# The section around the first five loads, synchronised by GpSimd in place of SyncE

## Chip, cores and metric

One core of a Trainium2 chip (trn2). The metric is device time in microseconds (us) of one execution; 298.03 us before, the median of three runs.

Engines are named as in the profile: PE is TensorE's matmul and PEld its weight load, DVE is VectorE, ACT ScalarE, POOL GpSimd, SP SyncE. A q behind a name (SPq, POOLq) stands for instructions that the engine's sequencer handles by itself: waits, no-ops, drains, branches and the issuing of transfers.

## What is computed

For every one of 8 batches and 12 heads, all dot products between 512 rows of x and 512 rows of y, each of 64 channels:

```python
def setup_inputs():
    batch, n_heads, seq_t, seq_s, channels = 8, 12, 512, 512, 64
    return {
        "x": np.random.randn(batch, n_heads, seq_t, channels).astype(np.float32),
        "y": np.random.randn(batch, n_heads, seq_s, channels).astype(np.float32),
    }

def reference(x: np.ndarray, y: np.ndarray) -> np.ndarray:
    return np.einsum('bhtc,bhsc->bhts', x, y).astype(np.float32)
```

Two inputs of 12.6 MB each are read and an output of 100.7 MB is written.

## The kernel before

**Tiling.** The 96 heads are taken in six groups of 16 (`NG` = 6). A group's x and y are each one load of 128 partitions by 4096 values (2 MB, `N` = 4096), so there are twelve loads: number 2g is x of group g, 2g + 1 is y of it. A head's 512 x 512 products make one result of 128 by 4096 floats (2 MB), in two halves of 2048, each from one of the two PSUM tiles `pm0` and `pm1`.

**Buffers.** Three buffers, `pair0` to `pair2`, hold two slots each. Five of the six slots (`SLOTS` = 5) take loads first and results later; the sixth holds group 1's inputs in bf16 at first. From the ninth result on, two results go out in one store of 4 MB from a pair.

**Stages of a group.** `compress` turns a landed load into bf16 (x by ACT into `xk`; y in four parts by DVE, POOL and ACT into `yb`), `mix` spreads x into `xb`, `transposes` on DVE makes `xT` and `yT`, PE makes the products in one loop (`all_products`), ACT copies them out of PSUM into slots (`copy`, line 140; the last result by DVE, line 142), and SP stores them (`transfer`, line 161).

**Who orders what.** Nearly all is ordered by hand: `emit` works out what an instruction has to wait for, puts the waits on its engine, and lets the instruction raise its engine's semaphore, or, for a transfer, the semaphore of its slot (`dma0` to `dma4`). All loads and nearly all stores are issued by SP on one DMA queue, in order; six pieces of one late store go by POOL's queue (`shares`).

**The beginning.** The framework opens the program with a barrier of all engines, in which POOL gathers the others' arrivals and then hands out the release (the trace puts it under line 430). Then comes the section that the change touches: `tc.tile_critical()`, line 367, in which five loads are issued (`load`, the issue itself is line 177). The section is a region that the framework's scheduler leaves alone; only the engines that have instructions in it, here SP, run into it. Around it the framework puts its own instructions, which the trace shows under lines 367 and 371: a no-op ahead of the section, which raises a semaphore; a branch into it that waits for this semaphore; behind the loads, on SP, a semaphore that SP raises, a drain that waits for that one and raises the first again, and a no-op that waits for the drain. The two no-ops stand in the queue of the section's synchronising engine, the argument `sync_engine`; where none is given, as here, they stand on SP. `tc.close()` ends the framework's part with a drain of all engines and two barriers (line 371), gathered by POOL again. All that follows is the hand-ordered part: the memsets of `xb` (line 378) and ACT's table load come first, then the first `compress`.

Of the kernel before, what the change touches and what calls it, by code (L numbers as in the profile page):

```python
# [9 lines left out]
def kernel(  # L10
# [13 lines left out]
    nc = tc.nc  # L24
# [148 lines left out]
    def load(n):  # L173
        i = loaded[n] = places[n]
        emit(
            "sp",
            lambda: nc.sync.dma_start(slots[i], (yv if n % 2 else xv)[n // 2]),  # L177
            writes=both(i),
            dma=i,
        )  # L180
# [183 lines left out]
            for part in range(4):  # L364
                mix(i + 1, "dve", part)

    with tc.tile_critical():  # L367
        for n in range(SLOTS):
            load(n)
    tc.close()  # L370
# [75 lines left out]
```

## Time and profile before

| what | value |
|---|---|
| median of three runs | 298.03 us (297.98 to 298.11) |
| the profiled execution's own time | 297.92 us |
| its span, first to last instruction | 296.1 us |
| granted TensorE clock, mean | 0.787 |
| busy: ACT, DVE, PE, POOL | 208.2, 158.0, 139.9, 59.5 us |
| bytes moved | 125.85 MB, 425 GB/s over the span |
| packets on SP's DMA queue, on POOL's | 5888, 288 |
| first load issued, first packet starts | 0.96 us, 1.99 us |
| first load landed (its semaphore complete) | 8.74 us |
| five loads' issue, each | 0.39 to 0.55 us |
| the closing barriers' last release | 4.30 us |

The span is measured from the first instruction to the last on the core; the execution's own time has some 1.8 us more around it. Starts are given from the span's beginning. The short instructions of the queues (no-ops, drains, waits) are read from the trace's instruction records, which have nanoseconds. A semaphore's update has a time of its own in the trace, apart from the instruction that makes it.

### The profile page before, as it was taken

What the parts mean: (1) busy time and instruction counts of PE and PEld (TensorE: products, weight loads), DVE (VectorE), ACT (ScalarE), POOL (GpSimd) and SP (SyncE); (2) the same over time, 40 slices, a digit from 0 to 9 for tenths busy, and PEclk for the clock granted to TensorE, in tenths of its full rate; (3) what the DMA queues carried; (4) which work ended last, traced back from release to release, by engine and by line L of the source; (5) the groups of instructions that cost most, each with busy time, mean ns of one, the idle gap of its engine ahead of it and who ended that gap; (6) DMA issues with size and microseconds to landing.
All of it is one profiled execution on the core that took longest, in us unless ns stands there. A gap on an engine that the chain in (4) does not pass through costs nothing.

```text
span 296.1 us, 1231 instructions
## 1 busy us (share of the span) xinstructions
PE 139.9 (47%) x404; PEld 37.9 (13%) x404; DVE 158.0 (53%) x76; ACT 208.2 (70%) x107; POOL 59.5 (20%) x29
## 2 busy tenths in 40 slices
PE   0000040437576557556654655577546646575400
PEld 0000010112111111111111111111111111121200
DVE  2167798899929594925808529258095240002600
ACT  1664666999999999666966696669666976684000
POOL 2399999992000000000000000000000000040000
PEclk9999995657779997778789776765798787756855
DMA  7999999999999999999999999999999999999998
GB/s 272 427 429 427 432 429 427 432 425 425 427 438 427 460 425 426 425 429 447 429 456 426 425 429 425 425 438 434 434 456 425 425 429 429 425 438 422 415 436 348
DMA packets 6178, 125.85 MB, mean 425 GB/s; under 512 B 896, under 2 KB 896, under 8 KB 932
## 3 DMA queue, kind: packets, MB, share of 16 engines
q1 hardware_dynamic: 5888, 125.03, 98.7%
q0 software_dynamic: 288, 0.80, 0.7%
q14 instruction: 2, 0.02, 0.0%
HBM read 25.17 MB, written 100.66 MB: 425 GB/s over the span
## 4 chain that ended last, share of the span: by engine, by line
DMA 56%; ACT 23%; PE 7%; issue 4%; DVE 3%; SPq 0%; ACTq 0%
DMA out_dram<-pair 43%; ACT pair L140 21%; DMA pair<-in_y_dram 7%; DMA pair<-in_x_dram 6%; PE pm L248 6%; DVE pair L142 3%; ACT xk L140 1%; PE pm L298 1%; ACT yb L140 1%; DVE xk L142 1%; SPq L177 0%; ACTq L92 0%; SPq L371 0%; SPq L367 0%
## 5 line engine op out<-in xcount | busy, mean ns | idle before, releaser
L248 PE MATMUL pm<-yT,xT 128*128 128x512 bf16 x384 | 136.6, 501 | 137.3 <-ACT pair L140 100.0
L140 ACT ACTIVATE pair<-pm 128x2048 f32<-128x2048 f32 x94 | 170.6, 1883 | 41.3 <-DMA out_dram<-pair 37.5
L225 DVE STREAM_TRANSPOSE xT<-xb 128x2048 uint32<-128x2048 uint32 x12 | 46.7, 3893 | 69.1 <-PE pm L248 66.7
L248 PEld LDWEIGHTS pm<-yT,xT 128*128 128x128 bf16 x384 | 36.0, 115 | 237.0 <-ACT pair L140 156.0
L161 POOL DMA_DIRECT2D out_dram<-pair x6 | 3.5, 583 | 193.7 <-ACT pair L140 193.7
L142 DVE COPY xb<-xk 32x2048 bf16<-32x2048 bf16 x32 | 41.7, 1304 | 0.9
L142 DVE CAST yb<-pair 64x2048 bf16<-64x2048 f32 x10 | 30.7, 3074 | 9.5 <-DMA pair<-in_y_dram 9.3
L140 ACT ACTIVATE xk<-pair 128x4096 bf16<-128x4096 f32 x5 | 18.1, 3617 | 10.4 <-DMA pair<-in_x_dram 10.3
L142 POOL COPY xb<-xk 32x2048 bf16<-32x2048 bf16 x8 | 23.5, 2939 | 6.7 <-ACT xk L140 6.2
L142 DVE COPY pair<-pm 128x2048 f32<-128x2048 f32 x2 | 4.5, 2286 | 31.9 <-PE pm L248 31.9
L234 DVE STREAM_TRANSPOSE yT<-yb 128x1024 uint32<-128x1024 uint32 x10 | 19.2, 1918 | 0.0
L140 ACT ACTIVATE yb<-pair 64x2048 bf16<-64x2048 f32 x5 | 12.4, 2472 | 3.9 <-DMA pair<-in_y_dram 3.8
L142 POOL CAST yb<-pair 64x2048 bf16<-64x2048 f32 x5 | 14.5, 2903 | 1.2 <-DMA pair<-in_y_dram 0.8
L142 POOL COPY xb<-pair 32x2048 bf16<-32x2048 bf16 x4 | 12.7, 3184 | 0.3
L140 ACT ACTIVATE pair<-pair 128x4096 bf16<-128x4096 f32 (+1 forms) x2 | 6.1, 3030 | 3.7 <-DMA pair<-in_x_dram 2.5
L142 DVE CAST pair<-pair 64x2048 bf16<-64x2048 f32 x2 | 5.4, 2694 | 4.0 <-DMA pair<-in_y_dram 4.0
L142 DVE COPY xb<-pair 32x2048 bf16<-32x2048 bf16 x4 | 5.2, 1306 | 0.1
L140 ACT ACT_TABLE_LOAD x1 | 1.3, 1283 | 4.4 <-PEq L371 4.4
L378 DVE MEMSET xb<- 128x2048 uint32 x1 | 1.8, 1765 | 4.9 <-PEq L371 4.9
L234 DVE STREAM_TRANSPOSE yT<-pair 128x1024 uint32<-128x1024 uint32 x2 | 3.9, 1946 | 0.0
L298 PE MATMUL pm<-yT,xT 128*16 128x256 bf16 (+5 forms) x20 | 3.3, 333 | 0.6 <-DVE pair L142 0.6
L142 POOL CAST pair<-pair 64x2048 bf16<-64x2048 f32 x1 | 3.3, 3293 | 0.1
(7 smaller groups left out, 5.8 us busy)
## 6 DMA issues: line engine op xcount, KB each, us to landing
out_dram<-pair SPq DMA_DIRECT2D x19, 4096.0 KB, 21.8
out_dram<-pair SPq DMA_DIRECT2D x9, 2048.0 KB, 9.3
pair<-in_x_dram SPq DMA_DIRECT2D x6, 2048.0 KB, 18.8
pair<-in_y_dram SPq DMA_DIRECT2D x6, 2048.0 KB, 16.5
out_dram<-pair SPq DMA_DIRECT2D x1, 1024.0 KB
out_dram<-pair POOLq DMA_DIRECT2D x2, 256.0 KB, 16.6
out_dram<-pair SPq DMA_DIRECT2D x2, 96.0 KB
out_dram<-pair POOLq DMA_DIRECT2D x2, 96.0 KB, 14.6
```

The lines of the kernel that those rows point to most:

```text
L140: lambda: nc.scalar.activation(dst, src, COPY)
L142: else engines[name].tensor_copy(dst, src),
L161: return engines[name].add_instruction(mybir.InstDMACopy(name=nc.get_next_instruction_name(), engine=engines[name].engine, ins=[place(src, ...
L225: lambda: nc.vector.transpose(xTs[half].rearrange("p (k r e) -> p k e r", k=K, e=E), xbs[half].rearrange("p (k e c) -> p k e c", k=K, e=E),),
L234: lambda: nc.vector.transpose(yTs[half].rearrange("p (r j) -> p j r", r=D), ybs[half][b].rearrange("p (j c) -> p j c", c=D),),
L248: last = nc.tensor.matmul(pms[k // 4][:, j, :], xT[:, k + j, h, :], yT[:, h * S:(h + 1) * S], start=True, stop=True,)
L298: last = nc.tensor.matmul(pms[0][:4 * c + 4, 2 * b + (lo - begin) // S, (lo - begin) % S:(lo - begin) % S + hi - lo], xT[:, lo // S, h, 32 ...
L378: lambda: engines[name].memset(xbs[half], 0.0),
```

## The change

One argument: the section gets GpSimd as its synchronising engine.

```diff
@@ -364,7 +364,7 @@
             for part in range(4):
                 mix(i + 1, "dve", part)
 
-    with tc.tile_critical():
+    with tc.tile_critical(sync_engine=nc.gpsimd.engine):
         for n in range(SLOTS):
             load(n)
     tc.close()
```

`load` still issues with `nc.sync.dma_start`, and the drain of the engine that ran in the section stays with that engine, SP.

## The prediction

> **What bounds the kernel now.** I read the page first, for which resource is full, then a table by stretches of the span, for where it is not full, then the start of the chain of waits, because the edit lies there, and last the rows of the two lines that the edit touches.
>
> The page says that the transfers fill the span:
>
> ```profile
> span 296.1 us, 1231 instructions
> ...
> DMA  7999999999999999999999999999999999999998
> ...
> q1 hardware_dynamic: 5888, 125.03, 98.7%
> ...
> HBM read 25.17 MB, written 100.66 MB: 425 GB/s over the span
> ```
>
> Of forty slices only the first and the last are under nine tenths, and SP's queue (q1) alone holds the 16 DMA engines for 98.7% of the span; ScalarE, the busiest engine, is at 70%. The view of busy time by stretch, with the DMA share and the rate as its last two columns, says where the rest lies:
>
> ```profile
> 0.00:2.00 2.00, 0.00 (x0) 0.00 (x0) 0.00 (x0) 0.00 (x0) 0.20 (x4) 1.00 0.03 8
> ...
> 3.00:294.00 291.00, 139.94 (x404) 37.94 (x404) 157.97 (x76) 208.24 (x107) 59.34 (x25) 0.79 1.01 431
> 294.00:296.10 2.10, 0.00 (x0) 0.00 (x0) 0.00 (x0) 0.00 (x0) 0.00 (x0) 0.50 0.14 55
> ```
>
> From 3 to 294 us the DMA share is 1.01, which is full, and in the packet records no single microsecond of that stretch is under 0.97. So the end is the start of the first load, plus a fixed 125.8 MB, plus a ragged tail of some 2 us. A change can only move the end through the stretch before 2 us, through the rate, or through the tail. The chain of waits, followed from its beginning (start, length, what), shows what fills that stretch:
>
> ```profile
> 0.67 0.05 issue
> 0.72 0.02 SPq L367
> 0.74 0.07 issue
> 0.80 0.03 SPq L371
> 0.84 0.12 issue
> 0.96 0.39 SPq L177
> 1.35 0.06 issue
> 1.41 0.41 SPq L177
> ```
>
> SP's queue leaves the opening barrier (its last wait runs from 0.654 to 0.671), runs a no-op of the section (0.719, line 367, it raises the section's semaphore), runs a branch that waits for that same semaphore (0.804, drawn under line 371), and issues the first load at 0.961. The first packet moves at 1.989, 1.03 us behind the issue. These no-op and branch are what the edit is about, so the rows of the two lines are the last view (durations min/median/max in ns, then first and last start):
>
> ```profile
> L367 SPq NOP  x2: 13/16/18, 0.7 to 3.7; - x2
> L367 SPq EVENT_SEMAPHORE  x1: 17/17/17, 3.5 to 3.5; - x1
> L367 SPq DRAIN  x1: 55/55/55, 3.5 to 3.5; - x1
> ```
>
> Two no-ops, one ahead of the section and one behind it, both on SP, with a drain between the loads and the second.
>
> **The change part by part.** The section's synchronising engine carries those two no-ops, so both go from SP to GpSimd's queue; five loads, drain and branch stay on SP, since the loads are still issued by SP, on SP's DMA queue. No DMA, no byte and no semaphore count of a compute instruction changes. What does change is that SP's branch waits for a semaphore that another engine raises.
>
> *The entry.* GpSimd hands out the release of the opening barrier at 0.612, and its next queue instruction, a drain under line 371, starts at 0.693. The no-op takes that place: 0.693 + 0.018 (the row of SP's no-op) = 0.711, and the update stands 2 to 3 ns behind an instruction's end in this trace (0.737 against 0.739 for SP's), so 0.714. Then the hop to SP. The trace has four rows of an engine that stands at a wait and is released by another's update: the release at 0.637 reaches SP at 0.654 (17 ns) and TensorE at 0.665 (28), the one at 3.924 reaches SP at 3.940 (16), and SP's last arrival at 3.796 reaches GpSimd at 3.820 (24). With 16 to 28 ns SP's branch starts at 0.730 to 0.742. It is 0.804 now, since SP runs its own no-op first and then needs 65 ns from the update (0.739) to the branch. So the first load, 157 ns behind the branch, comes 0.062 to 0.074 us earlier: I take 0.07, that is 0.89 in place of 0.961.
>
> Bounds of what the trace doesn't show, a no-op on GpSimd and its hop: below, SP can't start its branch ahead of 0.719, the start of its next instruction now, so the gain is at most 0.804 - 0.719 = 0.085. Above, the dearest GpSimd queue row that waits for no other engine is its drain of 0.179 us at 0.310, and the longest update-to-start of a wait is 76 ns (SP's second no-op: 3.594 to 3.670): 0.693 + 0.179 + 0.076 = 0.948, a loss of 0.14. The value taken goes by the cross-engine rows, which are the nearest in kind.
>
> [...]
>
> *The exit.* Behind the loads SP raises a semaphore (3.460), drains (3.537 to 3.592) and runs its no-op (3.670). Now the no-op waits on GpSimd's queue. Behind it there stand GpSimd's drain, its part of the closing barrier and the memset of xb1 (line 378), and all other engines wait in that barrier. GpSimd's queue steps are 79 to 81 ns apart (3.820, 3.899, 3.980). With the loads 0.07 earlier SP's drain ends at 3.52, the hop gives 3.55 for the no-op, 3.63 for the drain, 3.71 for the barrier's gathering wait; SP, one no-op shorter, arrives at about 3.65, ahead of it. That wait starts at 3.820 now, so the barrier ends some 0.11 earlier. This is worth nothing to the end, and the work that hides it is the first load:
>
> ```profile
> 4.43 1.28 ACT L140 ACT_TABLE_LOAD   x1 [4.43 <-PEq L371]
> 8.76 3.62 ACT L140 ACTIVATE xk<-pair 128x4096 bf16<-128x4096 f32 x1 [3.06 <-DMA pair<-in_x_dram]
> ```
>
> ScalarE has 3.06 us of idle time behind its table load, until load 0 has landed (8.74); VectorE's memset ends at 6.69 and its next instruction starts at 13.66. A barrier later by the dearest GpSimd row, 0.179, would be covered as well; only past 3.06 us would it cost its own length.
>
> *The sum.* Entry -0.07, exit 0, transfers 0: the profiled execution's span goes from 296.09 to 296.02, and its own time from 297.92 to 297.85. That execution is 0.11 under the median of the runs, 298.03, so the forecast in terms of the median is 298.03 - 0.07 = **297.96**. By the bounds alone, 297.95 to 298.17.
>
> **The rivals.** A difference of 0.2% is 0.60 us here, about what a measurement of this kernel can tell from no change.
>
> *The hop takes the saving.* If SP looks at the semaphore at 0.719, finds it not yet raised (0.714 plus its way), and sees it only after a wait as long as its own-semaphore rows, the branch starts 60 to 76 ns behind 0.714, at 0.774 to 0.790, and the gain is 0.01 to 0.03: 298.01. For it speaks that SP's three looks at its own semaphores cost that; against it that a waiting SP was released in 16 and 17 ns. [...]
>
> *GpSimd is late.* Its no-op could stand behind what is still in the engine. Its drain at 0.310 took 0.179 because four memsets were under way; these are done at 0.441, so little speaks for it. It gives the upper bound, 298.17.
>
> *The start-up lottery, slower.* Each DMA engine's first 16 KB packet took between 1.04 and 2.10 us (settled: 0.611), and since every engine is full from then on, what an engine loses there stays with it to the end. If other starting times give the engine that ends last a long first packet in place of a short one, the price is 2.10 - 1.04 = 1.06: 298.03 - 0.07 + 1.06 = 299.02. It decides from 0.67 us of extra delay on. Against it: the three runs lie within 0.13 us, so the draw looks repeatable, and the pattern of issues and their spacing stay as they are.
>
> *The same, faster.* If the delays fall so that all engines end together: in the packet records the engines have 1.14 us of mean work left after 294.0, while the last ends at 295.68, so levelling gives at most 1.68 - 1.14 = 0.54, and 297.42 with the entry's 0.07.
>
> *The change doesn't do what it says.* The no-ops might stay on SP: 298.03, told apart from the second case by the rows of line 367 alone; it goes with it below.
>
> **How the numbers follow.** The forecast 0.58, the saving lost in the hop (or the edit without effect) 0.21, GpSimd late 0.07, the lottery slower 0.07, faster 0.07. The first three, 0.86, all end within 0.2%; slower 0.07; faster 0.07. The likeliest case's own range is 297.95 to 298.17 by the bounds, and with the scatter of the runs (0.13) some 297.8 to 298.3. The range reaches into both lotteries, of which small draws are likelier than the full price, so I go to 0.4 below and 0.42 above the median shown: 297.6 to 298.45.
>
> **What would show it.** In the profile of the changed kernel line 367 should have its two no-ops in GpSimd's queue and none in SP's. SP's wait of the opening barrier to its first load, 0.307 now (0.654 to 0.961), should be 0.24; 0.28 to 0.30 is the hop rival, and above 0.31 GpSimd is late. The gathering wait of the closing barrier should start near 3.7. ScalarE's first idle time before load 0 should stay near 3 us, and the DMA share from 3 to 294 us at 1.01. I am wrong if that share falls or if the span moves by more than the first load does: then the rate or the tail was touched, and the first packets and the last ones of each engine are the place to look.

## The result and the profile after

The changed kernel takes 298.31 us, the median of 22 runs (298.15 to 299.42); the kernel before, run beside it, 298.01 us, also of 22 (297.83 to 298.29). The ratio is 1.0013, with a 95% interval of 1.0007 to 1.0019: slower by 0.30 us. That is 0.1%, but clear of no change, and in the direction opposite to the forecast.

The profile after, though, has the shorter span. Two lines of the changed kernel's page:

```profile
span 296.0 us, 1233 instructions
...
q1 hardware_dynamic: 5888, 125.03, 98.7%
```

The chain of waits of the changed kernel, cut to the first 3 us (start, length, what), shows the entry of the section:

```profile
0.55 0.06 issue
0.61 0.02 POOLq L430
0.63 0.06 issue
0.69 0.02 POOLq L367
0.72 0.02 issue
0.73 0.03 SPq L371
0.77 0.12 issue
0.89 0.39 SPq L177
...
```

The no-op (line 367) now runs on GpSimd's queue, and the chain crosses from there to SP's branch (line 371) in 0.02 us. In the trace's records the semaphore is raised at 0.717 and the branch starts at 0.733, 16 ns later; the first load is issued at 0.890 in place of 0.961, and its first packet moves at 1.907 in place of 1.989. The stretches of the changed kernel's span (last columns: DMA share, GB/s) look as they did:

```profile
0.00:2.00 2.00, 0.00 (x0) 0.00 (x0) 0.00 (x0) 0.00 (x0) 0.20 (x4) 1.00 0.21 49
...
3.00:294.00 291.00, 136.38 (x404) 37.34 (x404) 158.02 (x76) 208.20 (x107) 59.34 (x25) 0.84 1.00 431
294.00:296.00 2.00, 0.00 (x0) 0.00 (x0) 0.00 (x0) 0.00 (x0) 0.00 (x0) 0.50 0.14 57
```

431 GB/s through the middle, before and after. The first two microseconds hold more than before (49 in place of 8 GB/s), because the packets start earlier. So inside the span the change did what was forecast, and the time was lost where neither profile page looks: around the span. Every run has a time and a span, so this can be counted run by run (medians, time minus span):

| kernel | runs | span, mean | around the span, median (lowest to highest) |
|---|---|---|---|
| before, in the first three batches of experiments | 93 | 296.16 | 1.86 (1.79 to 2.16) |
| changed, first measurement | 22 | 296.1 | 2.23 (2.18 to 3.42) |
| changed, second measurement | 11 | 296.06 | 2.24 (2.17 to 2.29) |

Over all 33 runs of the changed kernel the mean span is 296.07, which is 0.08 under that of before (plus or minus 0.05, twice the standard error); around the span there are 0.37 us more (2.23 in place of 1.86). 0.37 - 0.08 = 0.29, the whole result but for rounding. Of the 93 runs before, 85 lie at 1.79 to 1.91 around the span and eight at 2.01 to 2.16; why these eight are longer isn't known, and they don't move the median.

One warning for reading the profile after: its own execution took 299.42 us, one of two long ones among the 22 (the other 299.11). They have the usual span, and 3.4 and 3.2 us around it. The second measurement has none such, so their extra microsecond is no part of the median; it comes back at the end of the experiments.

### The profile page after: what moved, and what is told of

Read it like the earlier page. It is cut to its first block, busy times and chain, and to the rows that moved or that the text cites. A ratio compares the mean times of both kernels' runs of the same rounds, so it can differ in the third digit from the quotient of the medians.

```text
span 296.0 us, 1233 instructions
## 1 busy us (share of the span) xinstructions
PE 136.4 (46%) x404; PEld 37.3 (13%) x404; DVE 158.0 (53%) x76; ACT 208.2 (70%) x107; POOL 59.5 (20%) x29
## 4 chain that ended last, share of the span: by engine, by line
DMA 60%; ACT 21%; PE 7%; issue 4%; DVE 2%; SPq 0%; ACTq 0%; POOLq 0%
DMA out_dram<-pair 46%; ACT pair L140 18%; DMA pair<-in_y_dram 7%; DMA pair<-in_x_dram 6%; PE pm L248 6%; DVE pair L142 2%; ACT xk L140 1%; ACT yb L140 1%; PE pm L298 1%; DVE xk L142 1%; SPq L177 0%; ACTq L92 0%; SPq L371 0%; POOLq L367 0%; POOLq L430 0%
## 5 line engine op out<-in xcount | busy, mean ns | idle before, releaser
L248 PE MATMUL pm<-yT,xT 128*128 128x512 bf16 x384 | 133.4, 492 | 140.4 <-ACT pair L140 103.4
```

Source lines behind the costliest of these rows:

```text
L248: last = nc.tensor.matmul(pms[k // 4][:, j, :], xT[:, k + j, h, :], yT[:, h * S:(h + 1) * S], start=True, stop=True,)
```

## The experiments

Twelve runs in four batches, each timed beside the kernel before on the same chip. GpSimd's queue has 64 instructions in the kernel before and 68 in the changed one (the whole program of the engine, branches and barriers included); SP's has 68 and 66. The profile's instruction records hold eight fewer of each: 56 and 60 on GpSimd, 60 and 58 on SP. The first batch asks which of these, or the handshake itself, costs the time.

**The changed kernel again**, without an edit.

> The changed kernel once more, for a second trace of it. Three theories of the 0.30 us that it loses. T1, the closing: the loss lies behind the span, in the program's end, because GpSimd's queue holds four instructions more (68 in place of 64). T2, the handshake: the waits between SP and GpSimd around the section cost it. T3: SP's queue is two instructions shorter (66 in place of 68), and that moves something. All three expect about 298.3 here, a span near 296.0 and so some 2.2 us around the span, where the kernel before has 1.83 in its profile. The first load should again be issued 0.07 us earlier than before, at 0.89.

298.29 (298.14 to 298.47) against 298.04, ratio 1.0006 (0.9997 to 1.0015); 2.24 around the span; the first load at 0.889. As expected by all three. Its trace gives the usual case of the changed kernel's end, used below.

**Four no-ops on GpSimd, SyncE as before.**

```diff
+    for _ in range(4):
+        nc.gpsimd.nop().then_inc(signal("pool"), 1)
+        record("pool", "pool", 1, (), ())
     for n in range(2 * NG):
         if n == 11:
```

> The kernel before, synchronised by SyncE as before, with four no-ops added to GpSimd's queue behind its first memset, where it waits 6 us anyway; its queue then has 68 instructions, as the changed kernel's. T1: the loss appears without the change, 2.2 us around the span and 298.4 in all, as the first load is not earlier here. T2 and T3: nothing, 1.83 around the span and 298.0.

298.38 (298.28 to 298.59) against 298.04, ratio 1.0011 (1.0002 to 1.0020), 2.25 around the span, mean span 296.17. The whole loss appears without the change, with no-ops that stand where GpSimd waits, and its first load is issued at 0.962 as before. T1 holds; the handshake (T2) isn't needed for it.

**SP's queue back to 68.** The two no-ops on SP also change the order in which semaphores are allocated, which saves GpSimd one of its five clearing instructions at the end; one no-op on GpSimd keeps its queue at 68. The changed kernel, with

```diff
+    for _ in range(1):
+        nc.gpsimd.nop().then_inc(signal("pool"), 1)
+        record("pool", "pool", 1, (), ())
+    for _ in range(2):
+        emit("sp", nc.sync.nop)
     for n in range(2 * NG):
```

> The changed kernel with two no-ops added to SP's queue and one to GpSimd's, so that SP has 68 instructions as before the change and GpSimd 68 as after it. T3: the loss goes, 297.95. T1 and T2: it stays, 298.3, with 2.2 us around the span.

298.32 (298.09 to 298.61), 2.22 around the span: the loss stays, and T3 falls.

**GpSimd's queue down to 66.** The changed kernel, with two semaphores allocated first, so that those cleared together at the end are numbered in a row and take three clearing instructions in place of five:

```diff
+    for p in ("dmapool", f"dma{LAST}"):
+        signal(p)
     with tc.tile_critical(sync_engine=nc.gpsimd.engine):
```

> The changed kernel with its semaphores allocated in another order, so that the end clears them in three instructions in place of five; GpSimd's queue has 66 instructions. T1, if it is a boundary between 66 and 68: the loss goes, 297.9 to 298.0 with 1.8 us around the span; if the boundary is at 65 or 66, or if each instruction costs, all or half of the loss stays (298.1 to 298.3). T2 and T3: 298.3, less at most 0.1 for the clears.

297.85 (297.67 to 298.11) against 298.04, ratio 0.9993 (0.9984 to 1.0002), 1.84 around the span: with two instructions fewer the loss is gone, and the first load is still issued 0.07 us earlier, at 0.890.

The second batch asks what kind of a price it is. First the number between:

```diff
-    for _ in range(4):
+    for _ in range(3):
```

> The kernel before with three no-ops more in GpSimd's queue, 67 instructions. 66 cost nothing and 68 cost 0.39 us behind the closing barrier. A step at a boundary: either 298.04 with 1.85 around the span, or 298.43 with 2.24, and nothing between. A cost of each instruction: 2.04 or so around the span.

298.28 (298.08 to 298.46) against 297.98, ratio 1.0007 (0.9998 to 1.0016), with 2.11 around the span (2.06 to 2.26). Neither theory had this: not all of the step, but far more than one instruction in four. 66 costs nothing, 67 costs 0.26 us, 68 costs 0.39.

**Longer queues.** The no-ops now stand behind GpSimd's last copy, where it has nothing to do until 262 us (its next transfer in the kernel before is issued at 262.35). One wait comes with them, so sixteen make 81:

```diff
+    for _ in range(16):
+        emit("pool", nc.gpsimd.nop)
     prepare(2)
```

> The kernel before with 17 more instructions in GpSimd's queue (81), put where it has nothing to do, behind its last copy. Step at a boundary that the end of the program has crossed: 2.24 around the span, the same as with 68, or less, if what has to be brought in for the end is now asked for earlier. A cost of each instruction: 3.5 or more around the span. Only a count of 67 or 68 that falls badly: 1.85.

298.39 (298.23 to 298.83) against 297.98, ratio 1.0014 (1.0005 to 1.0023), which looks like the same loss, and isn't: around the span it is 1.84 again, and the mean span is 296.55, 0.40 longer. The DMA view of this kernel from 290 to 293 us (queue, kind: packets, MB, share of 16 engines) says what has moved into the span:

```profile
core 0 of [0], span 296.5 us
...
DMA packets 37, 1.19 MB, mean 396 GB/s; under 512 B 0, under 2 KB 0, under 8 KB 0
...
q1 hardware_dynamic: 36, 1.18, 91.5%
q14 instruction: 1, 0.01, 0.6%
```

One packet of the instruction queue (q14), 8192 bytes, from 291.475 for 0.309 us in the packet records. In the kernel before two such packets stand in the span, at 116.2 and 161.1; this is a third. The last data packet ends at 296.00, against 295.68 in the profile of before; single profiles of the other kernels here have it between 295.43 and 295.84, so the 0.40 us of the mean span is the firmer figure.

With 100 in place of 16:

> The same with 101 more (165). If the 0.39 us is the wait for a block of instructions that GpSimd's program needs at its end, then the boundary now lies in the body of the kernel, far ahead of the end: the block comes in while GpSimd has nothing to do, an instruction transfer of 16 KB stands inside the span, and around the span it is 1.85 again, 298.0 in all. If it is a fixed price of a longer program: 2.24, 298.4.

298.13 (297.95 to 298.44) against 297.98, ratio 1.0003 (0.9994 to 1.0012); 1.84 around the span, mean span 296.31, 0.16 longer. The third instruction packet is in the span again, now at 75.4. The DMA view of this kernel from 75 to 76 us:

```profile
DMA packets 29, 0.45 MB, mean 451 GB/s; under 512 B 1, under 2 KB 1, under 8 KB 1
...
q1 hardware_dynamic: 28, 0.44, 104.4%
q14 instruction: 1, 0.01, 1.9%
```

A longer program by itself is not what costs the end: 101 more instructions leave the time around the span as it was. With 165 in the queue the packet comes at 75.4, with 81 at 291.5; what it follows is taken up below. It was expected with 16 KB, the size of a packet behind the changed kernel's span (at 298.450, below), and came with 8.

**SP's queue longer instead.**

```diff
+    for _ in range(4):
+        emit("sp", nc.sync.nop)
     for n in range(2 * NG):
```

> The kernel before with four more instructions in SP's queue (72) and one fewer in GpSimd's (63). If only GpSimd's queue is near its boundary: 1.85 around the span, 298.0. If any engine's longer queue costs the end: 2.24, 298.4.

298.03 (297.80 to 298.11) against 297.98, ratio 0.9999 (0.9990 to 1.0008), 1.85 around the span: four more on SP cost nothing (GpSimd's queue has 63 here, one clearing instruction fewer). Of the two queues made longer here, GpSimd's shows the loss and SP's, up to 72 instructions, does not; no run lengthened another engine's.

The third batch asks whether the version with 66 is a gain, and whether the step is the same for the changed kernel. The merged clears alone, in the kernel before:

> The kernel before, synchronised by SyncE, with the clears at the end merged (three in place of five), so GpSimd's queue has 62 instructions. If the gain of the changed kernel with 66 instructions came from the earlier first load: 298.0 here, span 296.15, 1.85 around it. If it came from the merged clears or a shorter queue: 297.85.

297.95 (297.78 to 298.13) against 297.98, ratio 0.9998 (0.9989 to 1.0007), 1.85 around the span, mean span 296.11: no effect that can be told.

The 66 once more:

> The changed kernel with the clears merged (66), once more, beside the same kernel before: again 297.85 to 297.95, the span some 0.1 shorter than before's, 1.84 around it. If its first measurement was chance: 298.0.

298.02 (297.72 to 298.23) against 297.98, ratio 1.0000 (0.9991 to 1.0009); 1.84 around the span. The loss is gone again, but this time the total shows no gain. The mean span is 296.12 against 296.14. Over both measurements (22 runs) it is 297.98 in the median and 296.07 in mean span, against 298.01 and 296.16 for before. That is the size of the earlier load, but the totals do not settle that this version beats the kernel before; that it removes the changed kernel's loss is settled.

And one no-op more on it:

> The same with one no-op in GpSimd's queue (67). If the step lies between 66 and 67 whoever synchronises the section: 2.1 around the span as with 67 in the kernel before, and some 298.15 in all. If the step belongs to one arrangement: 1.84 and 297.9.

298.17 (297.97 to 298.36) against 297.98, ratio 1.0005 (0.9995 to 1.0014), with 2.08 around the span (2.06 to 2.16). In the changed kernel the step is between 66 and 67. In the kernel before, 64 costs nothing and 67 costs 0.26; 66 was not run there, so the same step fits but is not pinned down as closely.

**Between 68 and 81.** The last run, with 11 in place of 16:

> The kernel before with 12 instructions more in GpSimd's queue (76), between 68, which lost 0.39 us behind the closing barrier, and 81, which lost nothing there but had an 8 KB instruction transfer inside the span at 291.5 us and a span 0.4 us longer. If the loss is a wait for that block, asked for when GpSimd comes to a fixed place of its program: the transfer is asked for earlier than with 68, so the loss around the span is under 0.39, 1.85 to 2.2 us, and the transfer shows behind 291.5 or not at all. If it is a fixed price beyond the step: 2.24 again.

298.44 (298.31 to 298.72) against 298.00, ratio 1.0015 (1.0006 to 1.0024), 2.34 around the span (2.31 to 2.40), mean span 296.13: the eleven no-ops do not lengthen the span, where sixteen in the same place do. So the loss is not smaller than with 68, against the first theory, and not 2.24 either. Its trace shows why, in the records behind the span, which hold the semaphore updates of the program's end. In the kernel before, updates of semaphore 2 begin there at 296.620, then 248 others are updated once each from 296.818 to 297.475, and semaphore 2 is updated nine times from 297.699 to 298.056. They are read here as a meeting of the engines, a clearing of the semaphores and a last barrier; the records hold the updates alone. Times in us, from the trace of one execution each:

```
kernel         span end   first update of the    last update of the   run's time minus
               (GpSimd)   end, after span end    last barrier         that last update
before (64)    296.093    0.527                  298.056              -0.136
after_gp66     296.253    0.527                  298.241              -0.131
before_gp67    296.147    0.527                  298.106              +0.144
before_gp4     296.074    0.526                  298.061              +0.259
after_again    296.242    0.527                  298.204              +0.266
before_gp76    296.373    1.019                  298.853              -0.133
before_gp81    296.512    0.526                  298.473              -0.133
before_gp165   296.527    0.527                  298.516              -0.136
```

The last column is -0.13 wherever nothing is lost at the very end (that it is negative says that the run's time does not begin and end exactly with these records). With 67 it is +0.14 and with 68 +0.26: 0.28 and 0.39 us are lost behind the last barrier. The two other profiles with 67 and 68, of after_gp67 and after_sp2, have +0.12 and +0.26. With 76 nothing is lost there, but the first step of the end comes 0.49 us late, and the 8 KB instruction packet stands at 297.458, just behind that delay. With 81 and 165 neither place is late, and the packet lies inside the span.

GpSimd's own instruction records show the delay itself inside the span of the two longest programs, always behind its 68th record. Times in us:

```
kernel         68th record ends   69th record starts   between them   the same step without it
before_gp165    70.977            71.414              0.437          0.079 (the other no-ops)
before_gp81    286.095            286.499              0.404          0.044 (in the kernel before)
before_gp76    296.373            (none: the span ends with the 68th record)
```

Both times GpSimd stands still for 0.36 us longer than that step takes elsewhere, at the same count of instructions and at different times. With 76 the same place is exactly the end of the span, and the next thing seen of the end is 0.49 us late. With 68, 67 and 66 in the queue the records end with the 60th, 59th and 58th, so the place lies 8, 9 and 10 instructions further, behind what is recorded.

So the numbers fit a pause of GpSimd at one fixed place of its program, which moves with the number of instructions ahead of it: from behind the last barrier (67, 68) to ahead of the end's first step (76) to inside the kernel (81, 165); that with 66 and fewer the program ends before it fits the times. Behind the barrier and at the end's first step 0.28 to 0.49 us are lost, so something seems to wait for GpSimd there, though the records don't show what; inside the kernel the 0.36 us are there as well, but GpSimd has time to spare behind them (its next transfer is issued at 263.0 with 165, its last clear waits for data until 296.5 with 81), so that they are covered.

What stays open: with 67 and 68 neither the pause nor the packet is in the records, which end with the last barrier, so that the loss there is the same event is inferred from its place and from how it moves. What GpSimd does in the pause can't be seen either. It is not a wait for the 8 KB packet: that comes 4.0 us behind the pause with 165, 5.0 us with 81, and with 76 behind the end's first update (297.458 against 297.392). That the packet belongs to GpSimd's program is inferred too, from its coming only with 76 and more; the records do not name its engine.

The two long runs of the changed kernel are another matter. In the one that was profiled, the last barrier comes 0.19 us later after the span than usual (its last update is 2.152 behind the span's end, 1.962 in after_again), a further 0.98 us is lost behind it, and there is a packet of 16 KB of kind instruction on another queue, from 298.450 for 1.219 us, which no other trace here holds. The other long run has no trace. Why they are longer wasn't found out.

## Why the prediction was wrong

**The bound: right for the span.** The DMA engines are full from 3 to 294 us (a share of 1.01 before, 1.00 after), and the span moved with the first load: 0.08 (plus or minus 0.05) in the mean of 33 runs for 0.07. That the one profiled execution came out at the forecast 296.02 is luck, as single spans of the changed kernel lie between 295.9 and 296.4. The working takes the end of the span for the end of the run ("So the end is the start of the first load, plus a fixed 125.8 MB, plus a ragged tail"), and there it left something out.

**The entry: right.** Forecast: GpSimd's no-op at 0.693, the update at 0.714, SP's branch at 0.730 to 0.742, the load 0.07 earlier, at 0.89. Measured: 0.694, 0.717, 0.733, 0.890. The hop took 16 ns, as the four cross-engine rows had it (the other engines' releases in these barriers lie in the same 16 to 28 ns). The rival by which SP sees GpSimd's update as late as its own (60 to 76 ns in the kernel before) did not come true: SP was released as fast as the engines that wait in the barriers. Whether it already stood at its wait can't be told, since the update at 0.717 and the 0.719 at which SP started its next instruction before lie too close together.

**The exit: wrong, at no cost.** The closing barrier was to start gathering 0.11 earlier, at 3.71, and starts at 3.835, where it was 3.820. The rows of line 367 in the changed kernel:

```profile
L367 POOLq NOP  x2: 13/13/13, 0.7 to 3.7; - x2
L367 POOLq EVENT_SEMAPHORE  x2: 17/17/17, 0.8 to 3.6; - x2
L367 SPq DRAIN  x1: 122/122/122, 3.5 to 3.5; - x1
```

I had moved two no-ops; GpSimd got two more instructions, one that raises a semaphore (0.771) and one that waits for SP's drain (3.625). SP lost the one that raised a semaphore and got a wait of its own (3.678), its drain took 122 ns in place of 55, and the fourth load's issue took 0.626 us in place of 0.547, so that the fifth is issued at 2.937, where it was 2.930. In the second trace of the changed kernel that issue took 0.585 and the barrier starts gathering at 3.795: still not 3.71. The cover held as said. The same ScalarE rows in the changed kernel:

```profile
4.45 1.28 ACT L140 ACT_TABLE_LOAD   x1 [4.45 <-PEq L371]
8.68 3.62 ACT L140 ACTIVATE xk<-pair 128x4096 bf16<-128x4096 f32 x1 [2.94 <-DMA pair<-in_x_dram]
```

The table load is 0.03 later (4.454 in place of 4.426), and 2.94 us of idle time still lie behind it.

**The sum: the step that failed.** "Entry -0.07, exit 0, transfers 0: the profiled execution's span goes from 296.09 to 296.02, and its own time from 297.92 to 297.85." The second half of the sentence carries the 1.83 us around the span over unchanged, with a term of nothing that isn't even written down. It measured +0.37, five times the saving, and turned the sign. The miscount at the exit was part of it: by the prediction GpSimd's queue grows by the two no-ops, which would have made 66, and 66 costs nothing; it grew by four. But the price of a queue's length was not in the working at all, and no rival named it. The prediction's signs of being wrong did not cover it either: they ask whether the DMA share falls or the span moves by more than the load, and neither happened. That 298.31 still lies inside the stated 297.6 to 298.45 is luck, for the range was drawn that wide for small draws of the start-up lottery, which did not come.

**The rivals.** "GpSimd is late" and "the hop takes the saving" fell with the load at 0.89, both lotteries with a mean span that moved by no more than the first load, and a DMA share that stayed (1.00 after 1.01). The no-ops did move, so the edit did what it says.

## What to carry to other kernels

The measured time has a part that no line of the profile's page covers; take it for each run (time minus span) before looking for a loss inside. Where an edit changes how many instructions an engine's queue holds, count them, those that a framework adds too, and look whether the count has a step in it. On GpSimd's queue 66 was free here (in the changed kernel), 67, 68 and 76 cost 0.26, 0.39 and 0.49 us at the end, and with 81 and 165 the span was 0.40 and 0.16 us longer; on SP's, 72 in place of 68 cost nothing. The step was found by adding three and four no-ops to the unchanged kernel, where they hide (2.11 and 2.25 us around the span in place of 1.85), and it was got around by saving two instructions elsewhere on that queue (1.84).

## What the runs showed of the hardware

- In two traces GpSimd paused for 0.36 us longer than the same step takes elsewhere, behind its 68th recorded instruction: at 71.0 us with 165 instructions in its queue, at 286.1 us with 81. Around the span both took 1.84 us, as before. With 76 that place was the end of the span, and 0.49 us more went by behind it.
- One instruction packet of 8 KB (0.309 us) more in the span, where SP's queue held the 16 DMA engines for 91.5% (with 81) and 104.4% (with 165), went with a longer mean span: 0.40 us with the packet at 291.5 us, 0.16 us with it at 75.4 us. With five no-ops fewer and the packet behind the span, the mean span was 296.13, as before. With 165 no run tells the packet's part from that of the hundred no-ops.
- A cross-engine release of a queue took 16 ns (GpSimd to SP, 0.717 to 0.733 in the changed kernel), less than the 60 to 76 ns from SP's update of its own semaphore to SP's next step in the kernel before (3.477 to 3.537, 0.739 to 0.804, 3.594 to 3.670).
- The time around the span mostly repeats better than the span: 85 of 93 runs of the kernel before lie between 1.79 and 1.91 us, the other eight between 2.01 and 2.16, while the spans of one kernel differ by up to 0.6 us.
